# A two-block transformer in fp32: two of three 256-column products become one of 512 columns, and the bias rows move to the weight queue

## The chip, the cores and the metric

The kernel runs on one core of one Trainium2 chip. The metric is device time in microseconds (us). The core's engines work side by side, each in the order of its own queue: TensorE (PE) multiplies matrices, VectorE (DVE) and ScalarE (ACT) work element by element, GpSimd (POOL) does small sums and starts some transfers, and SyncE (SP) starts nearly all transfers of weights.

## The reference

Two transformer blocks run one after the other on x[1, 256, 1024] in fp32. The first has two layers, each with two feed-forward parts around an attention:

```python
def swiglu(h, w_in, w_out):
    g, u = jnp.split(h @ w_in, 2, axis=-1)
    return (jax.nn.silu(g) * u) @ w_out

# first block, in each of its two layers (FFN_HIDDEN = 2816)
h = modulate(rms_norm(x, norm_g[layer, 0]), sh1, sc1)
x = x + 0.5 * g1[:, None, :] * swiglu(h, ffn_w_in[layer, 0], ffn_w_out[layer, 0])
...
# layer 0: differential attention, whose logits get a bias per head by distance
bias = jnp.take(table, t5_bucket(rel), axis=0)
...
x = x + 0.5 * g3[:, None, :] * swiglu(h, ffn_w_in[layer, 1], ffn_w_out[layer, 1])
```

The second block mixes by convolutions, attends to a memory, and ends with product-key experts: each token picks its best experts by two top-k steps over query scores, and sums gelu(u_e . h) * gate * v_e over those it picked. The kernel computes u_e . h for all experts, 128 at a time, and drops what was not picked by one-hot products.

## The kernel before

Activations lie feature-major: x is [128, 8, 256], 8 tiles of 128 features by 256 tokens. An fp32 operand is split into two fp32r parts, hi and lo, and one product is three matmuls of 256 columns, which `mm3` (L145 to L149) issues for each 128x128 weight: whi with hi (L147), whi with lo (L148), wlo with hi (L149).

Weights come by `pieces` (L100 to L110): 1 MB from SP's queue into a tile `raw` (three buffers, two among the experts), which is split in two pieces of 128x1024. ScalarE copies out `whi` (L115), VectorE subtracts `wlo` (L116), and each piece is eight weights for PE. There are four buffers each of whi and wlo (three among the experts).

`ffn` (L431) is called four times; f0 stands before the attention of layer 0 and ends at about 260 us, f1 follows that attention, f2 and f3 belong to layer 1. Its first product goes over 22 hidden tiles j: one load, one piece for the gate `og`, one for `ou`, then silu (L450), the product `pr` (L452) and its split into `ghi` and `glo` (L160, L161). Its second product goes over 8 output tiles n with 22 triples each and adds the result to x (L426). Behind it `Stat.add` squares each new tile of x on ScalarE (`sq`, L182), adds it up on POOL (`sqa`, L193), and PE sums over the partitions (`po`, L177) for the next norm.

`prepare_bias` (L495 to L531) builds layer 0's bias tile TB while f0 runs: VectorE writes the eight heads' lines `mrow` (L509), and POOL's queue copies them to DRAM (`line`, L511), copies each line 128 times (`rows`, L515), and reads the rows back skewed by one element per partition into TB (L517). It is a generator, and `ffn` takes a step of it at some j (`next(beside)`).

Transfers `araw` (L355) and their sums on VectorE (L358) prepare the modulation of coming layers and run in the background of the FFNs.

With the experts, `experts_u` (L986) takes 128 experts in two halves, each expert's product (8 triples) evacuated by gelu (L1095 for the first 64). While the first 64 run, VectorE does the top-k of the tokens (L1020 to L1081) until about 1608 us. The last stage, from about 1902, multiplies by v with matmuls of 512 columns (L1171).

A scheduler sets the order in which the instructions of each engine stand; each engine then takes them in that order.

Of the kernel before, what the change touches and what calls it, by code (L numbers as in the profile page):

```python
# [10 lines left out]
F32 = mybir.dt.float32  # L11
# [42 lines left out]
def forward(ctx: ExitStack, tc: tile.TileContext, io, out, tap=None):  # L54
# [95 lines left out]

    def tok(h, k, a=0, b=T):

        return h[0][:, k, a:b], h[1][:, k, a:b]
# [65 lines left out]
    def h_tiles():  # L219
        return (hp.tile([128, KT, TE], F32R, tag="hhi", name="hi"), hp.tile([128, KT, TE], F32R, tag="hlo", name="lo"))  # L220

    class Norm:
# [3 lines left out]
        def __init__(self, a, b=None, h=None):  # L226
            self.a, self.b = a, b
            self.h = h_tiles() if h is None else h
            if b is not None and h is None:
                hi, lo = (t[:, :, T:TE] for t in self.h)  # L230
                bb = b.unsqueeze(2).to_broadcast([128, KT, 2])
                act.activation(hi, bb, AF.Copy)
                dve.tensor_tensor(lo, bb, hi, op=ALU.subtract)
# [51 lines left out]
    def fm_one(p, h, h32=None, n=T):  # L285
        o = mm_bank([128, n])
        for k in range(KT):
            if len(p) == 1:
                pe.matmul(o, p[0][:, k * 128:(k + 1) * 128], h32[:, k, :], start=(k == 0), stop=(k == KT - 1))  # L289
                continue  # L290
            mm3(o, blk(p, k), tok(h, k, 0, n), k == 0, k == KT - 1)
        return o
# [138 lines left out]
    def ffn(f, norm, gate, following, more=None, done=False):  # L431

        with tc.tile_pool(name="ff", bufs=1) as fp:
            ghi = fp.tile([128, FKT, T], F32R, name="ghi")
            glo = fp.tile([128, FKT, T], F32R, name="glo")
            src = io[f"ffn_in{f}"]
            h = norm.h
            for j in range(FKT):
                if f == 0 and j in (4, 6, 8, 10, 12, 14):
                    next(beside)  # L440
                it = W.pieces(src[j])
                if j == 0 and not done:
                    og, ou = norm.pair(next(it), next(it))
                elif j < 2:
                    og, ou = fm_pair(next(it), next(it), h)
                else:
                    og = fm_one(next(it), h)
                    ou = fm_one(next(it), h)
                sg = work("sil", [128, T], bufs=2)
                act.activation(sg, og, AF.Silu)  # L450
                pr = work("pr", [128, T], bufs=2)
                dve.tensor_tensor(pr, sg, ou, op=ALU.mult)  # L452
                split_into(ghi[:, j, :], glo[:, j, :], pr)
                tick()
# [14 lines left out]
            for n in range(KT):  # L469
                o = mm_bank([128, T])  # L470
                for k in range(FKT):
                    mm3(o, next(wb), (ghi[:, k, :], glo[:, k, :]), k == 0, k == FKT - 1)
# [15 lines left out]
    nlam = tbp.tile([128, 1], F32, name="nlam")  # L488
    g08 = tbp.tile([128, 1], F32, name="g08")
# [5 lines left out]
    def prepare_bias():  # L495
# [14 lines left out]
        line = dram.tile([8, 384], F32, name="line")  # L510
        pool.dma_start(out=line, in_=mrow)  # L511
        for q in range(4):
            yield
            rows = dram.tile([2, 128, 384], F32, name=f"rows{q}")
            pool.dma_start(out=rows, in_=line[2 * q:2 * q + 2, :].unsqueeze(1).to_broadcast([2, 128, 384]))  # L515

            pool.dma_start(out=TB[:, 2 * q:2 * q + 2, :],  # L517
# [462 lines left out]
    MID = 64  # L980
    with tc.tile_pool(name="pe0", bufs=1) as p0:
# [4 lines left out]
        def experts_u(e0, e1, evac):  # L986
            for c in range(e0 // 2, e1 // 2):
                for i, p in enumerate(W.pieces(io["peer_u"][c])):
                    evac(2 * c + i, fm_one(p, h))

        with tc.tile_pool(name="tk", bufs=1) as tk:
# [102 lines left out]
            def evac0(i, o):  # L1094
                act.activation(S0[:, i, :], o, AF.Gelu)  # L1095
# [11 lines left out]
        with tc.tile_pool(name="pe1", bufs=1) as p1:  # L1107
# [49 lines left out]
            xtok = hp.tile([128, 2, D], F32, tag="hhi", name="xtok")  # L1157
# [176 lines left out]
```

## Time and profile before

| what | value |
|---|---|
| median of 3 runs | 2270.47 us (2269.82 to 2273.29) |
| the profiled execution | 2270.32 us, its span 2268.5 us |
| PE, weight loads (PEld) | 98%, 94% of the span |
| VectorE, ScalarE, POOL | 77%, 55%, 4% |
| DMA | 467.76 MB, 206 GB/s in the mean |
| mean granted clock of TensorE | 0.996 |

The span goes from the first instruction to the last. A share is busy time by the span, over stages with different limits. An engine's row says how much it worked, not whether anything waited for it; for that one goes to the waits and to short windows.

### The profile page before, as it was taken

Reading aid. Unit: us, or ns where it says so; the run is one execution under the profiler, and the core shown is the slowest. Engines: PE = TensorE matmul, PEld = TensorE weight load, DVE = VectorE, ACT = ScalarE, POOL = GpSimd, SP = SyncE. Lnnn points to the kernel's source line nnn. Section 1 sums busy time; section 2 is a strip of 40 time slices with the busy share of each in tenths; the row PEclk is TensorE's granted clock in tenths of the full one; section 3 lists DMA queues with packets and bytes.
Section 4 is the critical chain, followed back from the end, with each engine's and each line's share of the span. In section 5 each row is a group of like instructions: output and inputs, shape, how many; then the busy total and the mean of one; then the engine's idle time right before and its main releaser. Section 6 shows DMA issues by size and latency. Waiting matters only on the chain.

```text
span 2268.5 us, 42687 instructions
## 1 busy us (share of the span) xinstructions
PE 2229.0 (98%) x16748; PEld 2131.5 (94%) x16748; DVE 1739.7 (77%) x3501; ACT 1258.6 (55%) x2389; POOL 85.3 (4%) x89
## 2 busy tenths in 40 slices
PE   8999899999999999999999999999999999999998
PEld 8999898999999999999999999999999999888887
DVE  7878667977777787765799886999668997666665
ACT  5544477544654457545523555445567776555555
POOL 0100000000100020000100010000000000000000
PEclk9999899999999999999999999999999999999999
DMA  9887644777668763555444453345543434555554
GB/s 364 297 325 300 231 168 164 301 275 293 245 263 300 292 231 129 216 182 182 164 159 165 161 219 115 117 184 186 186 155 144 145 136 152 193 192 188 185 187 157
DMA packets 68377, 467.76 MB, mean 206 GB/s; under 512 B 9888, under 2 KB 10184, under 8 KB 12368
## 3 DMA queue, kind: packets, MB, share of 16 engines
q1 hardware_dynamic: 64608, 461.67, 54.9%
q0 software_dynamic: 3280, 2.84, 0.5%
q8 instruction: 132, 2.16, 0.4%
q14 instruction: 69, 0.57, 0.1%
q10 hardware_dynamic: 288, 0.52, 0.1%
HBM read 463.88 MB, written 2.63 MB: 206 GB/s over the span
## 4 chain that ended last, share of the span: by engine, by line
PE 92%; DVE 3%; ACT 3%; issue 1%; POOL 0%; DMA 0%; ACTq 0%; DVEq 0%; POOLq 0%
PE mm L149 22%; PE mm L147 22%; PE mm L148 22%; PE mm L1171 8%; PE lg L1171 8%; PE lg L1126 2%; PE mm L289 2%; PE po L177 1%; ACT whi L115 1%; DVE wlo L116 1%; DVE lo L238 0%; DVE lo L275 0%; DVE nt L270 0%; PE po L962 0%; ACT e L576 0%
## 5 line engine op out<-in xcount | busy, mean ns | idle before, releaser
L115 ACT ACTIVATE whi<-raw 128x1024 fp32r<-128x1024 f32 x696 | 733.9, 1059 | 624.2 <-PE mm L148 414.6
L116 DVE TENSOR_TENSOR wlo<-raw,whi 128x1024 fp32r<-128x1024 f32 x696 | 850.5, 1226 | 295.8 <-ACT whi L115 291.0
L147 PE MATMUL mm<-hi,whi 128*128 128x256 f32 x3144 | 900.2, 287 | 2.6 <-ACT hi L274 2.1
L149 PE MATMUL mm<-hi,wlo 128*128 128x256 f32 x3144 | 892.7, 284 | 1.3 <-DVE wlo L116 1.2
L148 PE MATMUL mm<-lo,whi 128*128 128x256 f32 x3144 | 887.2, 282 | 0.1
L147 PEld LDWEIGHTS mm<-hi,whi 128*128 128x128 f32 x3144 | 595.2, 190 | 5.0 <-ACT hi L274 2.6
L149 PEld LDWEIGHTS mm<-hi,wlo 128*128 128x128 f32 x3144 | 596.4, 190 | 3.0 <-DVE wlo L116 2.7
L148 PEld LDWEIGHTS mm<-lo,whi 128*128 128x128 f32 x3144 | 596.9, 190 | 1.8 <-DVE wlo L116 0.6
L149 PE MATMUL mm<-ghi,wlo 128*128 128x256 f32 x704 | 197.4, 280 | 0.0
L147 PE MATMUL mm<-ghi,whi 128*128 128x256 f32 x704 | 197.4, 280 | 0.0
L148 PE MATMUL mm<-glo,whi 128*128 128x256 f32 x704 | 197.4, 280 | 0.0
L358 DVE CUSTOM_DVE_ANT_0 araw<-araw,cb 128x1024 f32<-128x1024 f32 x160 | 191.4, 1225 | 1.0 <-ACT cb L407 1.0
L160 ACT ACTIVATE vph<-S 128x128 fp32r<-128x128 f32 x256 | 77.1, 302 | 131.9 <-PE lg L1171 131.8
L148 PEld LDWEIGHTS mm<-glo,whi 128*128 128x128 f32 x704 | 132.7, 188 | 0.0
L147 PEld LDWEIGHTS mm<-ghi,whi 128*128 128x128 f32 x704 | 132.7, 188 | 0.0
L149 PEld LDWEIGHTS mm<-ghi,wlo 128*128 128x128 f32 x704 | 132.7, 188 | 0.0
L161 DVE TENSOR_TENSOR vpl<-S,vph 128x128 fp32r<-128x128 f32 x256 | 73.4, 288 | 44.3 <-PE lg L1171 43.8
L824 DVE SCALAR_TENSOR_TENSOR cfc<-cf,vec,cfc 128x256 f32<-128x256 f32 x240 | 100.0, 490 | 0.0
L1118 DVE TENSOR_SCALAR ohA<-cst,sel 128x128 f32<-128x128 f32 x256 | 82.2, 342 | 21.8 <-PE lg L1126 20.8
L1171 PE MATMUL mm<-whi,vph 128*128 128x512 f32 x256 | 80.7, 395 | 0.2 <-ACT vph L160 0.2
L1171 PE MATMUL mm<-wlo,vph 128*128 128x512 f32 x256 | 80.9, 395 | 0.0
L1171 PE MATMUL lg<-whi,vpl 128*128 128x512 f32 x256 | 80.8, 395 | 0.0
(392 smaller groups left out, 3277.7 us busy)
## 6 DMA issues: line engine op xcount, KB each, us to landing
raw<-ffn_in SPq DMA_DIRECT2D x88, 1024.0 KB, 4.9
araw<-ada SPq DMA_DIRECT2D x72, 1024.0 KB, 6.9
raw<-peer_u SPq DMA_DIRECT2D x64, 1024.0 KB, 4.8
raw<-peer_v SPq DMA_DIRECT2D x64, 1024.0 KB, 4.8
raw<-ffn_out SPq DMA_DIRECT2D x44, 1024.0 KB, 4.8
araw<-kv_ada SPq DMA_DIRECT2D x8, 1024.0 KB, 6.8
raw<-w_cf SPq DMA_DIRECT2D x8, 1024.0 KB, 4.7
raw<-w_scx SPq DMA_DIRECT2D x8, 1024.0 KB, 4.8
```

The source lines that it names most:

```text
L115: act.activation(hi[:, :m], r, AF.Copy)
L116: last_split[0] = dve.tensor_tensor(lo[:, :m], r, hi[:, :m], op=ALU.subtract)
L147: pe.matmul(o, a[0], b[0], start=start, stop=False)
L148: pe.matmul(o, a[0], b[1], start=False, stop=False)
L149: pe.matmul(o, a[1], b[0], start=False, stop=stop)
L160: act.activation(pair_hi, src, func, **kw)
L161: dve.tensor_tensor(pair_lo, src, pair_hi, op=ALU.subtract)
L289: pe.matmul(o, p[0][:, k * 128:(k + 1) * 128], h32[:, k, :], start=(k == 0), stop=(k == KT - 1))
L358: dve.tensor_tensor_reduce(out=raw[:, i, :], in0=raw[:, i, :], in1=cb, scale=1.0, scalar=0.0, op0=ALU.mult, op1=ALU.add, accum_out=acc[:, ...
L824: dve.scalar_tensor_tensor(o, cf[:, i, j:j + T], w, o, op0=ALU.mult, op1=ALU.add)
L1118: dve.tensor_scalar(A, iota, sel3[:, 0, t:t + 1], sel3[:, 2, t:t + 1], op0=ALU.is_equal, op1=ALU.mult)
L1171: pe.matmul(acc[t][d], lh, rh[:, d * 512:(d + 1) * 512], start=s0, stop=s1)
```

## The change

`mm_wide` replaces `mm3` where hi and lo can lie side by side: one matmul of 512 columns takes whi with [hi | lo] into a bank [128, 2, 256], and one of 256 columns adds wlo with hi to its first half. The halves are then added in SBUF: ScalarE copies one out of PSUM, VectorE adds the other. It is used for j from 2 to 20 of each FFN's first product, for n from 0 to 6 of its second (there a second residual step on VectorE adds the half), and for experts 16 to 62. The operands h and g become one tile each with both halves. In `prepare_bias` the copy to DRAM (`line`) is left out: each `rows` is read straight from one partition of mrow, 128 times, by two transfers of 192 KB, on SP's queue, and so is each read into TB. The steps are taken at j from 3 to 12. The small tiles nlam and g08 move to another pool.

```text
lines of after that stand in the rows below:
L105 weight load, L369 araw, L549 rows, L553 TB, L115/L116 whi/wlo, L468 copy of og's half, L470 silu,
L471 copy of ou's half, L166 g (the hi part), L188 sq, L244 next operand
```

```diff
@@ -147,6 +147,12 @@
         pe.matmul(o, a[0], b[0], start=start, stop=False)
         pe.matmul(o, a[0], b[1], start=False, stop=False)
         pe.matmul(o, a[1], b[0], start=False, stop=stop)
+
+    def mm_wide(o, a, b, start, stop):
+
+        order = ((o, a[0], b), (o[:, 0, :], a[1], b[:, 0]))
+        for i, (oo, w, r) in enumerate(order if start else order[::-1]):
+            pe.matmul(oo, w, r, start=start and i == 0, stop=stop and i == 1, skip_group_check=True)
 
     def tok(h, k, a=0, b=T):
 
...
@@ -289,6 +296,13 @@
                 pe.matmul(o, p[0][:, k * 128:(k + 1) * 128], h32[:, k, :], start=(k == 0), stop=(k == KT - 1))
                 continue
             mm3(o, blk(p, k), tok(h, k, 0, n), k == 0, k == KT - 1)
+        return o
+
+    def fm_wide(p, h):
+
+        o = mm_bank([128, 2, T])
+        for k in range(KT):
+            mm_wide(o, blk(p, k), h[2][:, :, k, 0:T], k == 0, k == KT - 1)
         return o
 
     def proj_fm(W, name, h, consume, c0=0, c1=None, whole=(), h32=None, ahead=None, norm=None, wide=False):
@@ -431,26 +445,36 @@
     def ffn(f, norm, gate, following, more=None, done=False):
 
         with tc.tile_pool(name="ff", bufs=1) as fp:
-            ghi = fp.tile([128, FKT, T], F32R, name="ghi")
-            glo = fp.tile([128, FKT, T], F32R, name="glo")
+            g = fp.tile([128, FKT, 2, T], F32R, name="g")
             src = io[f"ffn_in{f}"]
             h = norm.h
             for j in range(FKT):
-                if f == 0 and j in (4, 6, 8, 10, 12, 14):
+                if f == 0 and 3 <= j <= 12:
                     next(beside)
                 it = W.pieces(src[j])
                 if j == 0 and not done:
                     og, ou = norm.pair(next(it), next(it))
                 elif j < 2:
                     og, ou = fm_pair(next(it), next(it), h)
-                else:
+                elif j == FKT - 1:
                     og = fm_one(next(it), h)
                     ou = fm_one(next(it), h)
+                else:
+                    og = fm_wide(next(it), h)
+                    ou = fm_wide(next(it), h)
                 sg = work("sil", [128, T], bufs=2)
-                act.activation(sg, og, AF.Silu)
                 pr = work("pr", [128, T], bufs=2)
-                dve.tensor_tensor(pr, sg, ou, op=ALU.mult)
-                split_into(ghi[:, j, :], glo[:, j, :], pr)
+                if 2 <= j < FKT - 1:
+                    act.activation(sg, og[:, 1, :], AF.Copy)
+                    dve.tensor_tensor(sg, og[:, 0, :], sg, op=ALU.add)
+                    act.activation(sg, sg, AF.Silu)
+                    act.activation(pr, ou[:, 1, :], AF.Copy)
+                    dve.tensor_tensor(pr, ou[:, 0, :], pr, op=ALU.add)
+                    dve.tensor_tensor(pr, sg, pr, op=ALU.mult)
+                else:
+                    act.activation(sg, og, AF.Silu)
+                    dve.tensor_tensor(pr, sg, ou, op=ALU.mult)
+                split_into(g[:, j, 0, :], g[:, j, 1, :], pr)
                 tick()
             tc.keep_in_program_order(act.preload_act_table(AF.Sqrt))
             s = mod(gate)
@@ -467,9 +491,17 @@
 
             wb = stream()
             for n in range(KT):
-                o = mm_bank([128, T])
+                two = n < KT - 1
+                o = mm_bank([128, 2, T] if two else [128, T])
                 for k in range(FKT):
-                    mm3(o, next(wb), (ghi[:, k, :], glo[:, k, :]), k == 0, k == FKT - 1)
+                    if two:
+                        mm_wide(o, next(wb), g[:, k], k == 0, k == FKT - 1)
+                    else:
+                        mm3(o, next(wb), (g[:, k, 0, :], g[:, k, 1, :]), k == 0, k == FKT - 1)
+                if two:
+                    dve.scalar_tensor_tensor(xT[:, n, :], o[:, 1, :], s[:, n:n + 1], xT[:, n, :],
+                                             op0=ALU.mult, op1=ALU.add)
+                    o = o[:, 0, :]
                 residual(n, o, s[:, n:n + 1], st, nxt)
                 if more is not None:
                     more.add(xT[:, n, :], scale=v("final_g", n))
@@ -485,8 +517,8 @@
     tbp = ask.enter_context(tc.tile_pool(name="tb", bufs=1))
     dram = ask.enter_context(tc.tile_pool(name="dr", bufs=1, space=bass.MemoryType.DRAM))
     TB = tbp.tile([128, 8, 256], F32, name="TB")
-    nlam = tbp.tile([128, 1], F32, name="nlam")
-    g08 = tbp.tile([128, 1], F32, name="g08")
+    nlam = const.tile([128, 1], F32, name="nlam")
+    g08 = const.tile([128, 1], F32, name="g08")
     qz = [tbp.tile([128, 2, 256], F32, name=f"qz{i}") for i in range(4)]
     for t in qz:
         pool.memset(t[64:128, 0, :], 0.0)
@@ -507,14 +539,18 @@
         pf = bank("lg", [8, 384])
         pe.matmul(pf, rb, oh, start=True, stop=True)
         dve.scalar_tensor_tensor(mrow, pf, -1.0, mrow, op0=ALU.mult, op1=ALU.add)
-        line = dram.tile([8, 384], F32, name="line")
-        pool.dma_start(out=line, in_=mrow)
+        copies = []
         for q in range(4):
             yield
             rows = dram.tile([2, 128, 384], F32, name=f"rows{q}")
-            pool.dma_start(out=rows, in_=line[2 * q:2 * q + 2, :].unsqueeze(1).to_broadcast([2, 128, 384]))
-
-            pool.dma_start(out=TB[:, 2 * q:2 * q + 2, :],
+            copies.append(rows)
+            for i in range(2):
+                hd = 2 * q + i
+                sync.dma_start(out=rows[i:i + 1], in_=mrow[hd:hd + 1, :].unsqueeze(1).to_broadcast([1, 128, 384]))
+        for q, rows in enumerate(copies):
+            yield
+
+            sync.dma_start(out=TB[:, 2 * q:2 * q + 2, :],
                            in_=bass.AP(tensor=rows.tensor, offset=rows.offset + 127,
                                        ap=[[383, 128], [128 * 384, 2], [1, 256]]))
         yield
@@ -978,6 +1014,7 @@
     wsk.close()
     NI = 128
     MID = 64
+    WIDE = 16
     with tc.tile_pool(name="pe0", bufs=1) as p0:
         W = Weights(pw, 2, 3)
         S0 = p0.tile([128, MID, T], F32, name="S0")
@@ -986,7 +1023,8 @@
         def experts_u(e0, e1, evac):
             for c in range(e0 // 2, e1 // 2):
                 for i, p in enumerate(W.pieces(io["peer_u"][c])):
-                    evac(2 * c + i, fm_one(p, h))
+                    e = 2 * c + i
+                    evac(e, fm_wide(p, h) if WIDE <= e < MID - 1 else fm_one(p, h))
 
         with tc.tile_pool(name="tk", bufs=1) as tk:
             wkp[0] = tk
@@ -1092,6 +1130,11 @@
             proj_fm(W, "w_peer_q", h, q_evac, norm=norm)
 
             def evac0(i, o):
+                if WIDE <= i < MID - 1:
+                    t = work("sum", [128, T], bufs=2)
+                    act.activation(t, o[:, 1, :], AF.Copy)
+                    dve.tensor_tensor(t, o[:, 0, :], t, op=ALU.add)
+                    o = t
                 act.activation(S0[:, i, :], o, AF.Gelu)
                 if qs:
                     scores()
```

Three places show how the order of the engines' rows moved. First SP's queue in f0's first product, after the change. The weight loads of j4 to j7 are raw_1060, raw_1117, raw_1178 and raw_1242.

```order
29 L105 DMA raw_1060<-ffn_in0 128x2048
30 L549 DMA rows0_1057<-mrow_798 128x1x384 x2
31 L549 DMA rows1_1114<-mrow_798 128x1x384 x2
32 L105 DMA raw_1117<-ffn_in0 128x2048
33 L369 DMA araw_1171<-ada0 128x2048
34 L549 DMA rows2_1175<-mrow_798 128x1x384 x2
35 L105 DMA raw_1178<-ffn_in0 128x2048
36 L369 DMA araw_1232<-ada0 128x2048
37 L549 DMA rows3_1239<-mrow_798 128x1x384 x2
38 L105 DMA raw_1242<-ffn_in0 128x2048
39 L553 DMA TB_736<-rows0_1057 128x2x256
40 L105 DMA raw_1297<-ffn_in0 128x2048
```

Before, in the same place (j4 is raw_1085, then raw_1151, raw_1224 and raw_1297):

```order
29 L105 DMA raw_1085<-ffn_in0 128x2048
30 L105 DMA raw_1151<-ffn_in0 128x2048
31 L355 DMA araw_1217<-ada0 128x2048
32 L105 DMA raw_1224<-ffn_in0 128x2048
33 L355 DMA araw_1290<-ada0 128x2048
34 L105 DMA raw_1297<-ffn_in0 128x2048
35 L105 DMA raw_1366<-ffn_in0 128x2048
```

The eight reads of mrow now stand ahead of the loads of j5, j6 and j7; before, SP's queue held only raw and araw there.

Second, ScalarE's row in f0. After the change, raw_1117 is the load of j5 and raw_1178 that of j6; sil_1104 and pr_1105 evacuate j4, sil_1161 and pr_1162 evacuate j5.

```order
88 L468 ACTIVATE sil_1104<-mm_1066 128x256
89 L470 ACTIVATE sil_1104<-sil_1104 128x256
90 L471 ACTIVATE pr_1105<-mm_1087 128x256
91 L166 ACTIVATE g_804<-pr_1105 128x256
92 L115 ACTIVATE whi_1119<-raw_1117 128x1024
93 L115 ACTIVATE whi_1140<-raw_1117 128x1024
94 L468 ACTIVATE sil_1161<-mm_1123 128x256
95 L470 ACTIVATE sil_1161<-sil_1161 128x256
96 L471 ACTIVATE pr_1162<-mm_1144 128x256
97 L166 ACTIVATE g_804<-pr_1162 128x256
98 L115 ACTIVATE whi_1180<-raw_1178 128x1024
99 L115 ACTIVATE whi_1201<-raw_1178 128x1024
```

Before, raw_1151 is the load of j5 and raw_1224 that of j6; sil_1070 and ghi with pr_1072 evacuate j3, sil_1145 and ghi with pr_1147 evacuate j4:

```order
82 L115 ACTIVATE whi_1153<-raw_1151 128x1024
83 L450 ACTIVATE sil_1070<-mm_1016 128x256
84 L115 ACTIVATE whi_1182<-raw_1151 128x1024
85 L160 ACTIVATE ghi_805<-pr_1072 128x256
86 L115 ACTIVATE whi_1226<-raw_1224 128x1024
87 L450 ACTIVATE sil_1145<-mm_1091 128x256
88 L115 ACTIVATE whi_1255<-raw_1224 128x1024
89 L160 ACTIVATE ghi_805<-pr_1147 128x256
```

Before, the splits of a j alternate with the evacuation of the j two before it; after, those of j5 and of j6 stand behind the whole evacuation of the j just before them, and those of j7 likewise.

Third, ScalarE's row at the end of f0's second product; sq is the square of a new tile of x, hi (and h) the operand of the next product. Before:

```order
139 L182 ACTIVATE sq<-xT 128x256
140 L237 ACTIVATE hi<-xT,mod_sc_2271 128x256
141 L115 ACTIVATE whi<-raw 128x1024 x3
142 L237 ACTIVATE hi<-xT,mod_sc_2271 128x256
143 L115 ACTIVATE whi<-raw 128x1024 x2
...
149 L115 ACTIVATE whi<-raw 128x1024 x3
150 L237 ACTIVATE hi<-xT,mod_sc_2271 128x256
151 L115 ACTIVATE whi<-raw 128x1024 x2
152 L182 ACTIVATE sq<-xT 128x256 x5
153 L198 ACTIVATE rstd<-po,eps_c 128x2
```

After:

```order
175 L115 ACTIVATE whi<-raw 128x1024 x3
176 L188 ACTIVATE sq<-xT 128x256
177 L244 ACTIVATE h<-xT,mod_sc_2043 128x256
178 L115 ACTIVATE whi<-raw 128x1024 x3
179 L188 ACTIVATE sq<-xT 128x256
180 L244 ACTIVATE h<-xT,mod_sc_2043 128x256
181 L115 ACTIVATE whi<-raw 128x1024 x3
182 L188 ACTIVATE sq<-xT 128x256
183 L244 ACTIVATE h<-xT,mod_sc_2043 128x256
184 L115 ACTIVATE whi<-raw 128x1024 x2
185 L188 ACTIVATE sq<-xT 128x256
186 L244 ACTIVATE h<-xT,mod_sc_2043 128x256
```

Before, three sq stand by their own n and five behind the last whi; after, each of the eight stands by its own n. In POOL's row the transfers of rows and TB, which before stood ahead of and between the sqa, are gone.

## Rows read from the trace of the kernel before

**Rows 1.** The page: busy time, chain that ended last, costliest groups.

```profile
PE 2229.0 (98%) x16748; PEld 2131.5 (94%) x16748; DVE 1739.7 (77%) x3501; ACT 1258.6 (55%) x2389; POOL 85.3 (4%) x89
...
PE 92%; DVE 3%; ACT 3%; issue 1%; POOL 0%; DMA 0%; ACTq 0%; DVEq 0%; POOLq 0%
PE mm L149 22%; PE mm L147 22%; PE mm L148 22%; PE mm L1171 8%; PE lg L1171 8%; PE lg L1126 2%; PE mm L289 2%; PE po L177 1%; ACT whi L115 1%; DVE wlo L116 1%; DVE lo L238 0%; DVE lo L275 0%; DVE nt L270 0%; PE po L962 0%; ACT e L576 0%
...
L116 DVE TENSOR_TENSOR wlo<-raw,whi 128x1024 fp32r<-128x1024 f32 x696 | 850.5, 1226 | 295.8 <-ACT whi L115 291.0
```

**Rows 2.** Busy us (x count) of PE, PEld, DVE, ACT, POOL; PEclk; DMA share; GB/s.

```profile
150.00:200.00 50.00, 50.00 (x420) 50.00 (x419) 38.10 (x56) 23.91 (x36) 0.00 (x0) 1.00 0.79 295
200.00:260.00 60.00, 60.00 (x517) 60.00 (x516) 47.15 (x63) 28.10 (x35) 3.00 (x3) 1.00 0.77 291
570.00:589.00 19.00, 19.00 (x162) 19.00 (x161) 13.19 (x16) 8.96 (x11) 2.05 (x3) 1.00 0.63 235
2000.00:2050.00 50.00, 50.00 (x217) 40.55 (x216) 30.94 (x54) 28.06 (x55) 0.00 (x0) 1.00 0.54 190
```

**Rows 3.** The same view, behind f0, f1 and f2, and inside the first.

```profile
260.30:287.20 26.90, 17.01 (x110) 15.89 (x109) 16.33 (x33) 9.52 (x20) 5.47 (x4) 0.75 0.34 134
589.90:603.40 13.50, 13.48 (x111) 13.22 (x111) 12.59 (x32) 8.27 (x17) 7.04 (x2) 1.00 0.49 192
831.00:845.60 14.60, 13.59 (x111) 13.12 (x110) 13.23 (x26) 8.17 (x15) 7.25 (x3) 1.00 0.59 221
266.10:274.20 8.10, 0.29 (x4) 0.08 (x2) 6.26 (x7) 3.62 (x7) 5.47 (x4) 0.71 0.76 307
269.50:282.00 12.50, 5.75 (x20) 4.84 (x21) 7.07 (x14) 3.01 (x8) 4.39 (x4) 0.50 0.22 85
```

**Rows 4.** Waits between 255 and 290 us: total, times, longest.

```profile
POOL sqa L193 <- ACT sq L182: 44.1, 1, 44.1
...
PE po L177 <- POOL sqa L193: 7.8, 1, 7.8
```

**Rows 5.** ScalarE's timeline in f0's first product: start, duration, instruction [idle before it].

```profile
98.41 1.06 ACT L115 ACTIVATE whi<-raw 128x1024 fp32r<-128x1024 f32 x1 [1.50 <-issue]
...
101.29 1.06 ACT L115 ACTIVATE whi<-raw 128x1024 fp32r<-128x1024 f32 x1 [1.55 <-PE mm L148]
104.15 1.06 ACT L115 ACTIVATE whi<-raw 128x1024 fp32r<-128x1024 f32 x1 [1.50 <-issue]
```

**Rows 6.** Groups by line, 70 to 260 us: busy, mean ns, idle before.

```profile
L452 DVE TENSOR_TENSOR pr<-sil,mm 128x256 f32<-128x256 f32 x22 | 9.2, 416 | 6.0 <-PE mm L149 5.6 <-ACT sil L450 0.5
L160 ACT ACTIVATE ghi<-pr 128x256 fp32r<-128x256 f32 x22 | 8.8, 400 | 0.0
L450 ACT ACTIVATE sil<-mm 128x256 f32<-128x256 f32 x22 | 8.0, 365 | 0.0
...
L426 DVE SCALAR_TENSOR_TENSOR xT<-mm,mod_gt,xT 128x256 f32<-128x256 f32 x7 | 3.4, 479 | 1.5 <-PE mm L149 1.5
```

**Rows 7.** Busy time by stretch: f0, f1, experts with the top-k.

```profile
1525.00:1608.00 83.00, 83.00 (x700) 83.00 (x700) 77.08 (x139) 44.99 (x65) 0.00 (x0) 1.00 0.50 179
...
75.00:198.00 123.00, 122.97 (x1021) 122.00 (x1021) 98.51 (x151) 61.76 (x90) 7.13 (x8) 1.00 0.87 318
425.00:525.00 100.00, 100.00 (x837) 100.00 (x837) 77.37 (x114) 46.75 (x71) 0.00 (x0) 1.00 0.81 301
```

**Rows 8.** The instruction that writes mrow.

```profile
L509 DVE SCALAR_TENSOR_TENSOR mrow<-lg,mrow x1: 539/539/539, 83.1 to 83.1; 8x384 f32<-8x384 f32 x1
```

**Rows 9.** A stretch in which the DMA engines were full, the same view.

```profile
615.60:618.10 2.50, 2.50 (x24) 2.01 (x23) 1.80 (x2) 1.82 (x3) 0.00 (x0) 1.00 1.01 410
```

**Rows 10.** DMA issues: count, KB each, median us to landing.

```profile
raw<-ffn_in SPq DMA_DIRECT2D x88, 1024.0 KB, 4.9
...
kA<-FT SPq DMA_DIRECT2D x1, 16.0 KB, 2.2
```

**Rows 11.** The stretch in which kA<-FT ran, the same view.

```profile
627.00:627.30 0.30, 0.30 (x4) 0.30 (x4) 0.00 (x0) 0.30 (x3) 0.00 (x0) 1.00 0.23 55
```

More of the change, by code (lines that the diff above doesn't have):

```diff
@@ L219, in h_tiles @@
     def h_tiles():
-        return (hp.tile([128, KT, TE], F32R, tag="hhi", name="hi"), hp.tile([128, KT, TE], F32R, tag="hlo", name="lo"))
+        t = hp.tile([128, 2, KT, TE], F32R, tag="h", name="h")
+        return t[:, 0], t[:, 1], t
     class Norm:
@@ L229, in __init__ @@
             if b is not None and h is None:
-                hi, lo = (t[:, :, T:TE] for t in self.h)
+                hi, lo = (t[:, :, T:TE] for t in self.h[:2])
                 bb = b.unsqueeze(2).to_broadcast([128, KT, 2])
@@ L1154, in forward @@
                 done[0] += 1
-            xtok = hp.tile([128, 2, D], F32, tag="hhi", name="xtok")
+            xtok = hp.tile([128, 2, D], F32, tag="h", name="xtok")
             for t in range(2):
```

## The prediction

> **What bounds the kernel now.** I read the page first: TensorE (PE) is busy 98% of the span, and in the chain that ended last it has 92%, nearly all of it the three products of an fp32 triple, L147 to L149 [rows 1]. So time goes only in three ways: a shorter PE step, less idle PE, or new idle PE. Second, the step. A matmul record lasts 0.28 us at a step of 0.12 us, so about two of a window's count lie over its edge, and I take two off. In an FFN's first product that gives 50/418 = 119.6 ns, in f0's second 60/515 = 116.5, in f1's second 19/160 = 118.8; a matmul of 512 columns, in the last stage, 50/215 = 232.6 ns, which is 2 x 116.3 [rows 2]. The experts have 83/698 = 118.9 [rows 7]. Third, the idle. The largest piece lies behind f0: from the last FFN product, 260.3, the next two pairs of products take 26.9 us, where they take 13.5 behind f1 and 14.6 behind f2; between 266.1 and 274.2 PE has 0.29 us of work, and then runs at a granted clock of 0.50, its lower level (1.2 of 2.4 GHz), until 282 [rows 3]. The waits name the cause: PE's sum of squares (po, L177) waits 7.8 us for POOL's sqa (L193), and POOL had waited 44.1 us for ScalarE's sq (L182) [rows 4]. In the order of before, five sq stand behind the last weight split. Last, the cover: in f0 weights are split some 6 us before PE wants them: j4's last product ends at about 101.25, where the second split of j6 is released by it, and the first one of j6 started at 98.41 [rows 5].
>
> **The change, part by part.**
>
> *The wait behind f0.* In the order of after, the sq of each n stands right behind its own residual, as in f1, and no bias transfer stands in POOL's row. The stretch should take what f1 and f2 take: 26.9 - 13.5 or - 14.6 = 12.3 to 13.4 us. I take a gain of **12.7**.
>
> *Wide products.* 4 x 19 x 16 = 1216 triples of the first products, 4 x 7 x 22 = 616 of the second (154 of them f0's), 47 x 8 = 376 of the experts become one matmul of 512 and one of 256 columns: 2208 in all. If the wide one keeps the last stage's step and the narrow one its own, a triple saves 2 x 119.6 - 232.6 = 6.6 ns in the first products, 5.0 in f1 to f3's second and the experts, 0.4 in f0's second: 8.0 + 2.3 + 1.9 + 0.1 = 12.3 us. At the least it saves nothing: f0's second product runs 256 columns at 116.5, so the columns and not the number of instructions set the pace, and what makes 119.6 elsewhere may stay; the forecast would then be 2285. If the narrow one also falls to 116.3, a triple takes 348.9 and the sum is 18.4 us. No row decides between them, so I take **7.5**, a little over half of 12.3.
> The Trainium skill, "TensorE: Matmul & The Clock Gate", section "Back-to-back issue gap", gives each matmul its columns and a fixed small gap of about 2.5 ns. By it each merged pair would save that gap, 2208 x 2.5 = 5.5 us as an estimate; the trace's 232.6 against 2 x 116.5 shows no such gap.
>
> *Halves added.* In the FFNs a j gets two more copies on ScalarE and two more adds on VectorE (0.42 us each, as pr [rows 6]). VectorE stands at 98.5 of 123 us in f0 and 77.4 of 100 in f1; with 0.84 us in each 5.7 that becomes 93% and 92% [rows 7]. It stays below full and is covered by the splits' lead: **0.5 us** lost (0 to 24, see the rivals). The second residual step on VectorE, 28 x 0.48 us (L426 [rows 6]), lies under 15 us of PE work each: nothing.
> With the experts the cover is gone. From 1525 to 1608 VectorE, with the top-k, is busy 77.1 of 83 us [rows 7]. In it, 29 experts (16 to 44) get an add from PSUM of 0.42 us, as pr: 12.1 us, so 89.2 us must go into 83. What is late is wlo, and so PE: some 6 us; I take **6.5** lost (3, if the top-k ends some experts later, to 10).
>
> *The order in f0.* In after, ScalarE's splits for j5, j6 and j7 stand behind the whole evacuation of the j before. When PE ends j4, nothing is split for j5: copy 0.36, add 0.42, product 0.42, g 0.40, then whi 1.06, of which PE can use one matmul before wlo (1.22 later) [rows 1, 5, 6]: 2.7 + 0.9 = 3.6 us of idle PE, three times: **10.8 us lost** at the least. Behind f0 a gap of 8 us was followed by 12 us at the lower clock [rows 3]; these gaps are shorter, and I add 1 us for each, 3 (0 to 5).
>
> *Bias rows on the weight queue.* Eight reads, each 128 times one 1.5 KB line of one partition of mrow (192 KB), now stand in SP's queue: four ahead of j5's weights, two ahead of j6's, two of j7's. mrow is done at 83.1 + 0.5 [rows 8], and j4's weights have to pass too: they start at about 84. Behind them up to j7 are three weight loads and two ada loads, each 1.05 MB / 0.41 = 2.56 us at the most that the queues moved [rows 9]: 12.8 us. Then 2.2 us to landing, as of a 16 KB transfer [rows 10], and whi and wlo, 2.1. With R for one read, j7 can start at 84 + 8R + 12.8 + 2.2 + 2.1 = 101.1 + 8R. Without stalls it would at 101.25 + 2 x 5.75 = 112.7 (5.74 from the first split of j6 to that of j7 [rows 5]). The stall up to j7 is 8R - 11.6, where this is more than the 10.8 of the order; the two run at once, so the larger counts. They part at R = 2.8 us.
> R stands nowhere in the trace. Below, 192 KB at 410 GB/s: 0.5 us. Above, if one partition gives no more than one of the 16 DMA engines moves, 410/16 = 26 GB/s: 7.7 us. The nearest row is a transfer that holds to one partition, kA<-FT, 16 KB into one: the queues moved 55 GB/s in the 0.3 us in which it ran [rows 11]. At that, R = 196.6/55 = 3.6 us, and the stall is 17.0 us. I take it, with 3.5 us for the clock.
> The four TB transfers (256 KB, 0.6 us each at 410 GB/s) come behind, when the splits have a lead of 5.7 us again: nothing. Their cover gone, they would cost 2.6.
>
> **Sum**, against the profiled run's 2270.32 us (2268.5 of span and 1.8 around; the median of the runs is 2270.47): -12.7 - 7.5 + 0.5 + 6.5 = -13.2; + 17.0 + 3.5 = +7.3: **2277.6 us**.
>
> **Rivals.**
> A, the reads are quick (R under 2.8): only the order counts, -13.2 + 10.8 + 3 = +0.6, 2270.9 us. For it speaks that 16 KB may show a lag and not a pace.
> B, faster: the narrow matmul falls to the last stage's pace as well, and the wide products save 18.4 us and not 7.5. With quick reads that is +0.6 - 10.9 = -10.3, 2260.0 us; it decides from a saving of 12.6 us on, which brings A's sum to 4.5 us under before. For it: f0's second product (116.5) and the last stage (232.6) show that the pace can be had for either width. Against it: three of four FFN products, and the experts, don't run at it with the same instructions.
> C, one partition gives 26 GB/s: R = 7.7, stall 50 us, clock 5: +41.8, 2312 us. The Trainium skill, "SBUF — State Buffer", section "Door 1: The DMA port swizzle", measures 27.6 GB/s for transfers held to partitions 0 to 3, one port; by it R would be 7.1 us and the time 2307, as estimates. The 55 GB/s of kA speaks against it, though for writes of a twelfth of the size.
> D, VectorE becomes the pace of the FFNs: at 92 to 93%, if one of the two adds of a j falls out of the cover, 57 j of f0 to f2 cost 57 x 0.42 = 24 us. With A, 2294 us. For it: wlo already waits for whi; against it: the lead of two pieces.
>
> **How the numbers follow.** The forecast has 0.34, A 0.18, B 0.30, C 0.12, D 0.06. The time is the forecast's, 2277.6. From 2256 (B, with the top-k at 3) to 2308 (just under C's upper end) about 0.85 is held; by itself the forecast has 2270 to 2290 (R from 2.8 to 5). About 0.2%, 4.5 us, is what a measurement of this kernel can tell from no change. Slower has most of the forecast, C and D: 0.47; same A and the forecast's low end, 0.21; faster B and a little of A, 0.32.
>
> **What the profile after would show.** If the reads hold the queue: to landing of some 4 us or more each, ScalarE's whi waiting for DMA between 98 and 130, and PE idle ahead of j5, j6 and j7; if only the order counts, three gaps of 3.6 us with whi waiting for ScalarE's own row. Behind f0 the two pairs should take 13 to 15 us with no wait for sqa. In the FFNs, a wide step near 232 ns, narrow 116 to 120. In the top-k stage, wlo ahead of PE's waits and VectorE over 95%. The forecast is wrong if R is under 2.8 us, or if the FFNs run steadily slower or faster than the 349 to 359 ns of a triple.

## The result, and the profile after

The changed kernel takes **2285.26 us** (median of 4 runs, 2283.78 to 2285.69) against 2271.38 for the kernel before, run beside it (2269.82 to 2273.29): a ratio of 1.006, with a 95% interval of 1.0042 to 1.0077. It is slower by some 14 us, inside the range and on the side that was forecast (2277.6), but by twice the forecast 7 us. The profiled execution took 2284.82 us with a span of 2283.0, 14.5 over that of before.

The page of the kernel after, its busy times and its chain, to set beside [rows 1]:

```profile
PE 2218.3 (97%) x14540; PEld 2020.9 (89%) x14540; DVE 1822.4 (80%) x3728; ACT 1328.1 (58%) x2588; POOL 82.3 (4%) x80
...
PE 87%; DVE 6%; ACT 3%; DMA 2%; issue 1%; POOL 0%; ACTq 0%; DVEq 0%; POOLq 0%; SPq 0%
PE mm L155 31%; PE mm L149 10%; PE mm L147 10%; PE mm L148 10%; PE mm L1214 8%; PE lg L1214 8%; PE lg L1169 2%; PE mm L296 2%; DMA raw<-ffn_in 2%; DVE wlo L116 2%; ACT whi L115 1%; PE po L183 1%; DVE h L282 0%; DVE h L245 0%; DVE nt L277 0%
```

PE has 2208 matmuls fewer and less busy time, and yet the span grew: the chain has lost 5% of PE to others, 2% of it a transfer of weights, raw<-ffn_in, where transfers had 0% before. So PE stood idle, and the waits say where. Waits of the kernel after from 60 to 260 us (engine and line, what it waited for, total us, times, longest):

```profile
PE mm L155 <- ACT whi L115: 31.2, 6, 17.4
...
ACT whi L115 <- DMA raw<-ffn_in: 23.1, 4, 14.4
```

PE waited 31.2 us for whi in f0, and ScalarE, which makes whi, 23.1 for the weights (raw). What the transfers did meanwhile stands in stretches of f0, in the columns of [rows 2]:

```profile
84.00:96.00 12.00, 12.00 (x71) 10.41 (x70) 9.66 (x20) 7.98 (x15) 0.00 (x0) 1.00 0.86 27
111.50:118.00 6.50, 1.27 (x2) 0.74 (x3) 1.44 (x2) 2.00 (x2) 0.00 (x0) 0.50 1.00 339
118.00:126.00 8.00, 7.18 (x31) 6.01 (x30) 3.94 (x7) 1.19 (x3) 0.00 (x0) 0.75 0.86 31
126.00:132.00 6.00, 0.00 (x0) 0.00 (x0) 0.97 (x3) 0.77 (x2) 0.00 (x0) 0.73 0.97 316
132.00:141.00 9.00, 8.09 (x29) 6.65 (x30) 5.41 (x9) 2.46 (x4) 0.00 (x0) 0.61 0.90 107
```

From 84 to 96 the DMA engines are 86% busy and move 27 GB/s: these are the reads of mrow. When they are through, the weights come at 339 GB/s while PE stands still (1.27 of 6.5 us), at the lower clock (a granted clock of 0.50); then two more reads, and the same again. In three stretches PE works at the lower clock:

```profile
101.50:122.00 20.50, 5.27 (x15) 4.26 (x16) 4.65 (x6) 2.00 (x2) 0.00 (x0) 0.50 0.91 127
128.80:139.00 10.20, 6.09 (x18) 4.88 (x19) 4.99 (x8) 2.00 (x2) 0.00 (x0) 0.50 0.94 195
145.80:152.70 6.90, 5.03 (x15) 4.01 (x16) 4.36 (x4) 4.01 (x4) 0.00 (x0) 0.51 0.99 392
```

That is 16.4 us of work, about half of which, 8 us, is the price of the clock (an estimate: the level is half of the other). VectorE's split of g (L167) dates each j; its timeline from j4 to j8 (start, duration):

```profile
101.06 0.43 DVE L167 TENSOR_TENSOR g<-pr,g 128x256 fp32r<-128x256 f32 x1 [0.48 <-ACT g L166]
...
127.06 0.43 DVE L167 TENSOR_TENSOR g<-pr,g 128x256 fp32r<-128x256 f32 x1 [0.48 <-ACT g L166]
...
143.64 0.43 DVE L167 TENSOR_TENSOR g<-pr,g 128x256 fp32r<-128x256 f32 x1 [0.48 <-ACT g L166]
...
157.87 0.42 DVE L167 TENSOR_TENSOR g<-pr,g 128x256 fp32r<-128x256 f32 x1 [0.48 <-ACT g L166]
...
164.19 0.41 DVE L167 TENSOR_TENSOR g<-pr,g 128x256 fp32r<-128x256 f32 x1
```

The same split (L161) started in before at 103.5, 109.3, 115.0, 120.8 and 126.5; the first and the last of them:

```profile
103.53 0.42 DVE L161 TENSOR_TENSOR glo<-pr,ghi 128x256 fp32r<-128x256 f32 x1
...
126.51 0.42 DVE L161 TENSOR_TENSOR glo<-pr,ghi 128x256 fp32r<-128x256 f32 x1
```

So j4 was 2.5 us early, and j5 to j8 were 17.8, 28.6, 37.1 and 37.7 late: 40.2 us were lost from j4 to j8, 31.2 of them in waits and about 8 by the clock. Part of it came back. The busy times behind f0, in f1's first and second product, with the top-k, and in the last stage, to set beside [rows 2], [rows 3] and [rows 7]:

```profile
297.00:310.40 13.40, 13.38 (x111) 13.12 (x110) 11.27 (x27) 8.31 (x17) 0.00 (x0) 1.00 0.51 193
475.00:525.00 50.00, 50.00 (x286) 43.27 (x285) 45.27 (x76) 30.44 (x54) 0.00 (x0) 1.00 0.80 292
555.00:585.00 30.00, 30.00 (x175) 26.40 (x174) 25.15 (x33) 14.13 (x20) 3.90 (x3) 1.00 0.75 275
1540.00:1624.00 84.00, 81.00 (x450) 68.03 (x449) 81.34 (x160) 51.37 (x88) 0.00 (x0) 1.00 0.48 165
2000.00:2050.00 50.00, 50.00 (x220) 41.03 (x219) 31.55 (x56) 28.28 (x55) 0.00 (x0) 1.00 0.55 190
```

The two pairs behind f0 take 13.4 us where they took 26.9 [rows 3]. In f1's first product 284 matmuls (two less than the count) are 142 wide pairs in 50 us, 352 ns for what three of 119.6 did in 359; in its second 173 in 30 us, 347 ns. With the top-k VectorE is at 97% and PE no longer full. In the last stage, whose code is the same, 218 matmuls of 512 columns pass in 50 us and not 215 [rows 2].

The whole of the 14.5 us, by dated instructions of both traces (us, after less before):

| stretch | forecast | measured |
|---|---|---|
| up to j4 of f0 | 0 | -2.5 |
| j4 to j8, the held queue, order and clock | +20.5 | +40.2 |
| the rest of f0 | | -1.0 |
| the wait behind f0 | -12.7 | -13.6 |
| from there to the same place behind f3 | | -8.8 |
| from there to the last stage, with the experts | +6.5 | +5.4 |
| the last stage, from its first matmul | 0 | -5.2 |

The forecast had -7.5 for the wide products and +0.5 for their adds in all stretches together.

### The profile page after: what moved, and what is told of

The parts are those of the page before. It is cut to its first block, busy times and chain, and to the rows that moved or that the text cites. A ratio compares the mean times of both kernels' runs of the same rounds, so it can differ in the third digit from the quotient of the medians.

```text
span 2283.0 us, 38606 instructions
## 1 busy us (share of the span) xinstructions
PE 2218.3 (97%) x14540; PEld 2020.9 (89%) x14540; DVE 1822.4 (80%) x3728; ACT 1328.1 (58%) x2588; POOL 82.3 (4%) x80
## 4 chain that ended last, share of the span: by engine, by line
PE 87%; DVE 6%; ACT 3%; DMA 2%; issue 1%; POOL 0%; ACTq 0%; DVEq 0%; POOLq 0%; SPq 0%
PE mm L155 31%; PE mm L149 10%; PE mm L147 10%; PE mm L148 10%; PE mm L1214 8%; PE lg L1214 8%; PE lg L1169 2%; PE mm L296 2%; DMA raw<-ffn_in 2%; DVE wlo L116 2%; ACT whi L115 1%; PE po L183 1%; DVE h L282 0%; DVE h L245 0%; DVE nt L277 0%
## 5 line engine op out<-in xcount | busy, mean ns | idle before, releaser
L155 PE MATMUL mm<-h,whi 128*128 128x512 f32 x1592 | 555.1, 401 | 31.2 <-ACT whi L115 31.2
L147 PE MATMUL mm<-h,whi 128*128 128x256 f32 (+1 forms) x1552 | 449.9, 291 | 0.7 <-ACT h L281 0.6
L149 PE MATMUL mm<-h,wlo 128*128 128x256 f32 (+1 forms) x1552 | 441.2, 285 | 1.2 <-DVE wlo L116 0.9
L148 PE MATMUL mm<-h,whi 128*128 128x256 f32 (+1 forms) x1552 | 438.4, 283 | 0.6 <-DVE h L282 0.5
L155 PE MATMUL mm<-h,wlo 128*128 128x256 f32 x1592 | 418.7, 283 | 3.8 <-DVE wlo L116 3.7
L155 PEld LDWEIGHTS mm<-h,whi 128*128 128x128 f32 x1592 | 290.7, 191 | 90.2 <-ACT whi L115 33.7
L155 PEld LDWEIGHTS mm<-h,wlo 128*128 128x128 f32 x1592 | 302.6, 191 | 23.7 <-DVE wlo L116 8.1
L148 PEld LDWEIGHTS mm<-h,whi 128*128 128x128 f32 x1552 | 293.6, 189 | 2.8 <-DVE h L282 1.9
L149 PEld LDWEIGHTS mm<-h,wlo 128*128 128x128 f32 x1552 | 293.7, 189 | 2.5 <-DVE wlo L116 2.1
L147 PEld LDWEIGHTS mm<-h,whi 128*128 128x128 f32 x1552 | 293.6, 189 | 2.3 <-ACT h L281 0.8
L155 PE MATMUL mm<-g,whi 128*128 128x512 f32 x616 | 213.5, 393 | 0.0
L155 PE MATMUL mm<-g,wlo 128*128 128x256 f32 x616 | 168.0, 280 | 0.0
L155 PEld LDWEIGHTS mm<-g,whi 128*128 128x128 f32 x616 | 113.9, 188 | 23.9
L155 PEld LDWEIGHTS mm<-g,wlo 128*128 128x128 f32 x616 | 116.0, 188 | 2.3
L167 DVE TENSOR_TENSOR vpl<-S,vph 128x128 fp32r<-128x128 f32 x256 | 73.6, 290 | 38.1 <-PE lg L1214 38.0
```

What stands on the lines that cost most here:

```text
L147: pe.matmul(o, a[0], b[0], start=start, stop=False)
L148: pe.matmul(o, a[0], b[1], start=False, stop=False)
L149: pe.matmul(o, a[1], b[0], start=False, stop=stop)
L155: pe.matmul(oo, w, r, start=start and i == 0, stop=stop and i == 1, skip_group_check=True)
L167: dve.tensor_tensor(pair_lo, src, pair_hi, op=ALU.subtract)
```

## The experiments

The theory was that the eight reads, each of one partition, are slow and hold the weight queue. Its rivals: the packets are slow from wherever they are read; the wide products or the order of ScalarE's row lose the time.

**The shift of the tiles alone.** The change also moves two small tiles to another pool, and with them the tiles that lie behind them in SBUF. The 64 bytes, and the 32 of a later run, are reckoned from the layout; no view shows addresses. In the kernel before:

```diff
-    nlam = tbp.tile([128, 1], F32, name="nlam")
-    g08 = tbp.tile([128, 1], F32, name="g08")
+    nlam = const.tile([128, 1], F32, name="nlam")
+    g08 = const.tile([128, 1], F32, name="g08")
```

> The kernel before, with one thing of the change: the small tiles nlam and g08 lie in the other pool, so that all later tiles lie 64 bytes further on. Theory: the last stage, whose code is unchanged, fell from 232.4 to 228.9 ns per matmul of 512 columns by this shift alone; then its step is 229 here, the stage is 4.8 us shorter, f0's second product goes from 116.5 to about 118 ns and that of f1 to f3 from 118.8 to about 117.3, and the time is 4 to 8 us under before (2263 to 2267). Rival: the last stage gained by something else that the change does (another order, other transfers); then the step stays 232.4 and the time within 2 us of before.

It took 2266.57 us against 2270.68, a ratio of 0.9981 (0.9972 to 0.999). Its windows, in f0's second product, in f1's, and in the last stage:

```profile
200.00:258.00 58.00, 58.00 (x492) 58.00 (x492) 44.83 (x62) 26.48 (x33) 3.01 (x3) 1.00 0.76 284
571.00:589.00 18.00, 18.00 (x154) 18.00 (x153) 12.38 (x15) 8.39 (x11) 1.81 (x2) 1.00 0.65 240
2000.00:2050.00 50.00, 50.00 (x220) 41.00 (x220) 31.05 (x55) 28.85 (x56) 0.00 (x0) 1.00 0.53 191
```

The last stage has 218 matmuls in 50 us (229.4 ns), as the kernel after, and f0's second product 58/490 = 118.4 ns in place of 116.5. f1's, 18/152 = 118.4, did not fall to 117.3. From its first matmul to its last, the last stage takes 353.2 us and not 358.5, while the stages up to it take 1.5 us more. So the shift gives some 4 us, and it gives them in the last stage.

**The wide products alone.** The kernel after, with `line`, `rows` and TB on POOL's queue, and their steps at the j, as in before:

```diff
-                if f == 0 and 3 <= j <= 12:
+                if f == 0 and j in (4, 6, 8, 10, 12, 14):
...
+        line = dram.tile([8, 384], F32, name="line")
+        pool.dma_start(out=line, in_=mrow)
...
-                sync.dma_start(out=rows[i:i + 1], in_=mrow[hd:hd + 1, :].unsqueeze(1).to_broadcast([1, 128, 384]))
...
+            pool.dma_start(out=rows, in_=line[2 * q:2 * q + 2, :].unsqueeze(1).to_broadcast([2, 128, 384]))
```

> The kernel after, with the bias rows back on POOL's queue as before: the wide products alone (with the shift of the tiles). Theory, that the weight queue held behind the eight reads of mrow: the 40 us between j4 and j8 are gone, the wait behind f0 is back (13.7), so 14.5 - 40.1 + 13.7 + 2.4 = 9.5 us under before, about 2262. Rival, that the wide products and their additions lengthen f0: some 20 us and more of the loss stay between j4 and j8 and the time is above 2271.

2259.16 us, a ratio of 0.9949 (0.9934 to 0.9964). From 60 to 300 us PE's sum of squares (po) waits 7.8 us for sqa, as in [rows 4], and PE never waits for whi; its longest waits:

```profile
PE po L183 <- POOL sqa L199: 7.8, 1, 7.8
PE mm L147 <- ACT h L281: 2.1, 2, 1.5
```

The wide products lose nothing in f0: its last product ends at 257.6 us, where it ended at 260.6 before.

**The bias rows alone.** The kernel before, with the new `prepare_bias` and its steps at j from 3 to 12:

```diff
-                if f == 0 and j in (4, 6, 8, 10, 12, 14):
+                if f == 0 and 3 <= j <= 12:
...
-        line = dram.tile([8, 384], F32, name="line")
-        pool.dma_start(out=line, in_=mrow)
...
+                sync.dma_start(out=rows[i:i + 1], in_=mrow[hd:hd + 1, :].unsqueeze(1).to_broadcast([1, 128, 384]))
```

> The kernel before, with only the bias rows moved to the weight queue, all products as before. Theory of the held queue: 40.1 us lost between j4 and j8, 2.4 won ahead of it, 13.7 won behind f0: 24 us over before, about 2295; reads of mrow run at 27 to 28 GB/s, 7.0 us each. Rival, the order of ScalarE's rows with wide products made the loss: 10 to 14 us lost at j5 to j7, 13.7 won, about 2270.

2295.38 us, a ratio of 1.0107 (1.0091 to 1.0122): 24.7 us lost, as the theory had it. Its wait in f0 and the stretch of the first reads:

```profile
PE mm L147 <- ACT whi L115: 31.8, 7, 16.8
...
84.00:96.00 12.00, 12.00 (x102) 12.00 (x101) 9.02 (x16) 7.83 (x13) 0.00 (x0) 1.00 0.85 27
```

PE waits 31.8 us for whi, from 84 to 96 the queues move 27 GB/s again, and the two pairs behind f0 take 13.4 us. So this part alone makes the loss and the gain behind f0. ScalarE's new order comes with it too: its row there has whi of j5 (116.43) behind the whole evacuation of j4 (ghi, 101.27), after 14.7 us of waiting for the transfer.

**The same reads from 16 partitions.** The kernel after; the small product writes each head's line into 16 partitions, eight apart, and a read takes its 128 copies from them:

```diff
-        mrow = tbp.tile([8, 384], F32, name="mrow")
+        mrow = tbp.tile([128, 384], F32, name="mrow")
...
-                sync.dma_start(out=rows[i:i + 1], in_=mrow[hd:hd + 1, :].unsqueeze(1).to_broadcast([1, 128, 384]))
+                sync.dma_start(out=rows[i].rearrange("(r s) c -> r s c", s=8),
+                               in_=mrow[hd:128:8, :].unsqueeze(1).to_broadcast([16, 8, 384]))
```

> The kernel after, with each head's line in 16 partitions, eight apart (mrow is 128 x 384, the small product writes each line 16 times), and each read taking its 128 copies from these 16: same bytes, same packets, same queue, same order. Theory, that the one partition limits the read: a read falls from 7.0 us to 1 us or less, the stretch moves above 100 GB/s, the loss between j4 and j8 falls from 40 to what the order leaves, 11 to 14 us, and the time is 2257 to 2261. Rival, that packets of 1.5 KB or the writes into DRAM on this queue are slow by themselves: the stretch stays near 28 GB/s and the time near 2285.

2261.47 us, a ratio of 0.9958 (0.9943 to 0.9973), just over the upper end of what was expected. The stretch of its reads, and that behind it:

```profile
84.40:88.40 4.00, 4.00 (x25) 3.48 (x24) 4.00 (x7) 3.97 (x7) 0.00 (x0) 1.00 1.07 229
100.00:130.00 30.00, 20.55 (x81) 16.23 (x80) 18.95 (x29) 11.58 (x18) 0.00 (x0) 0.80 0.54 197
```

The reads now pass at 229 GB/s, and rows<-mrow lands in 6.0 us in the median and not 20.7. Same bytes, same packets, same queue: what made them slow was that each had its source in one partition (whether the partition itself is the limit, or a port that several share, this run does not separate). Between j4 and j7 16.3 us are still lost, 2 more than the 11 to 14 expected, with three gaps in which PE waits for whi (9.4 us) and ScalarE's row shows whi in its new place behind g, with no wait for a transfer before it:

```profile
101.84 0.42 ACT L166 ACTIVATE g<-pr 128x256 fp32r<-128x256 f32 x1 [0.95 <-DVE pr L473]
102.17 1.99 ACT L115 ACTIVATE whi<-raw 128x1024 fp32r<-128x1024 f32 x2
...
112.83 0.42 ACT L166 ACTIVATE g<-pr 128x256 fp32r<-128x256 f32 x1 [0.95 <-DVE pr L473]
113.15 1.99 ACT L115 ACTIVATE whi<-raw 128x1024 fp32r<-128x1024 f32 x2
...
123.47 0.42 ACT L166 ACTIVATE g<-pr 128x256 fp32r<-128x256 f32 x1 [0.95 <-DVE pr L473]
123.79 3.88 ACT L115 ACTIVATE whi<-raw 128x1024 fp32r<-128x1024 f32 x4
```

The 16.3 are the difference of the splits of g, 1.2 us early at j4 and 15.1 late at j7. From 100 to 130 the granted clock is 0.80 in the mean: in three stretches at 0.50 PE did 13.1 us of work (3.4, 3.2 and 6.5), half of which, some 6.5 us, is the clock's share (an estimate).

**The reads on POOL's queue.** The kernel after, with the slow reads, and TB, on another queue:

```diff
-                sync.dma_start(out=rows[i:i + 1], in_=mrow[hd:hd + 1, :].unsqueeze(1).to_broadcast([1, 128, 384]))
+                pool.dma_start(out=rows[i:i + 1], in_=mrow[hd:hd + 1, :].unsqueeze(1).to_broadcast([1, 128, 384]))
...
-            sync.dma_start(out=TB[:, 2 * q:2 * q + 2, :],
+            pool.dma_start(out=TB[:, 2 * q:2 * q + 2, :],
```

> The kernel after, with the same eight reads from one partition of mrow each, and the TB reads, on POOL's queue and no longer on the weight queue. Theory, that a slow read holds only what stands behind it on its own queue: the reads still take about 7 us each, 84 to 140 us, but the weights pass at their pace, PE doesn't wait for whi in f0 (under 2 us), five sq stand behind the last whi again, and the time is that of the wide products alone, 2257 to 2261. Rival, that the reads hold the DMA engines for all queues: weights land late in f0, PE waits 15 us and more there, time above 2272.

2298.99 us, a ratio of 1.0127 (1.011 to 1.0144): the rival was right. Its waits from 60 to 260 us:

```profile
ACT whi L115 <- DMA raw<-ffn_in: 46.6, 2, 43.5
...
PE mm L155 <- DVE pr L472: 38.3, 1, 38.3
```

ScalarE's timeline at that place, with the idle time before the instruction in brackets:

```profile
140.90 1.06 ACT L115 ACTIVATE whi<-raw 128x1024 fp32r<-128x1024 f32 x1 [43.53 <-DMA raw<-ffn_in]
```

And the stretch of the reads, in the columns of [rows 2], with what each queue had of it (packets, MB, share of the 16 DMA engines; q0 is POOL's, q1 SP's):

```profile
85.00:140.00 55.00, 20.35 (x116) 17.34 (x114) 14.18 (x26) 9.82 (x17) 3.99 (x7) 0.70 0.97 97
...
q0 software_dynamic: 593, 1.86, 81.3%
q1 hardware_dynamic: 476, 3.45, 15.4%
```

The wait of PE is put down to VectorE's pr, which had only to wait its turn: ScalarE's row shows the cause, whi waiting 43.5 us for a transfer on the other queue. From 85 to 140 the DMA engines are 97% busy and move 97 GB/s in the mean, and POOL's queue has 81% of their time for the smaller part of the bytes. So a place in the weight queue is not needed for the loss: here the slow reads held the DMA engines from another queue. (On POOL's queue the trace has the reads in packets of 3 and 4.6 KB; so packets of 1.5 KB are not what makes them slow.)

**Spread reads on POOL's queue, TB on the weight queue.** The kernel of the spread reads, with the reads on POOL's queue, which also brings back ScalarE's order of before:

```diff
-                sync.dma_start(out=rows[i].rearrange("(r s) c -> r s c", s=8),
+                pool.dma_start(out=rows[i].rearrange("(r s) c -> r s c", s=8),
```

> The kernel after, with the lines spread over 16 partitions as in the run before, the reads of mrow on POOL's queue and only the TB reads on the weight queue. In its order the splits of j5 to j7 stand ahead of the evacuations again, and all eight sq by their own n. Theory, that the order of ScalarE's row makes the 16 us left in f0 with the spread lines, and the five late sq the wait behind f0: neither is there, 2259.2 - 13.7 = 2245.5, 2243 to 2248. Rival, that the 16 us come from the weights' being late behind TB and rows: 10 us and more of them stay, 2255 or above.

2244.47 us, a ratio of 0.9885 (0.9869 to 0.9902). From 60 to 300 us no wait of PE is longer than 0.6 us, neither for whi nor for sqa. In the spread reads on the weight queue whi never waited for a transfer from 60 to 260 us, so it was the order that made the 16.3 us.

**And no adds beside the top-k.** The same, with the experts 16 to 45 as triples again:

```diff
-    WIDE = 16
+    WIDE = 46
```

> As the run with lines spread, reads on POOL's queue and TB on the weight queue, and the experts 16 to 45 as 256-column triples again, so that no add stands beside the top-k. Theory, that VectorE is full there: the 5.5 us lost between 1519 and 1657 us in the run with the wide products alone are not lost, 2239 to 2242. Rival, that they are lost to the wide products' own step or to ScalarE's copies: within 2 us of the same kernel with wide experts.

**2240.06 us**, a ratio of 0.9867 (0.9851 to 0.9884), under both kernels. It is 4.4 us under the run before it. The same stretch in that run and in this one:

```profile
1500.00:1584.00 84.00, 80.91 (x448) 68.02 (x447) 81.38 (x158) 51.32 (x89) 0.00 (x0) 1.00 0.47 165
...
1500.00:1584.00 84.00, 84.00 (x708) 84.00 (x707) 77.50 (x135) 45.59 (x68) 0.00 (x0) 1.00 0.52 176
```

VectorE falls from 97% to 92% and PE is full. In the run before, PE waits 3.0 us for VectorE's wlo between 1510 and 1645, in this one never. The edit takes out the wide products, ScalarE's copies and VectorE's adds at once, so it does not tell adds from copies: VectorE itself waited 15.1 us for the copies there.

**A shift of 32 bytes.** The first experiment left open by what rule the shift acts; this moved nlam alone, in the kernel before:

```diff
-    nlam = tbp.tile([128, 1], F32, name="nlam")
+    nlam = const.tile([128, 1], F32, name="nlam")
```

> The kernel before, with only nlam in the other pool: all later tiles lie 32 bytes further on, and the operands of most products, 96 bytes over a multiple of 128 before, lie on a multiple. Theory, that the step depends on where the operand lies and is short on the multiple (f0's second product, whose ghi lay on one, had 116.5 ns, the others 118.8 to 119.6): the first products of the FFNs fall to about 116.5, 4 x 1056 x 3.1 ns = 13 us less there, the last stage to 229 or under, and the time is 2250 to 2256, while f0's second product rises to 118. Rival, that 64 bytes matter by another rule (the last stage alone): first products stay at 119 to 120 and the time within 5 us of before.

2273.39 us, a ratio of 1.001 (1.0001 to 1.002). A miss for the theory: the first products kept 50/418 = 119.6 ns, f0's second went to 58/483 = 120.1, the last stage to 50/214 = 233.6:

```profile
150.00:200.00 50.00, 50.00 (x420) 50.00 (x419) 38.73 (x57) 24.02 (x37) 0.00 (x0) 1.00 0.78 297
200.00:258.00 58.00, 58.00 (x485) 58.00 (x485) 45.22 (x62) 26.39 (x32) 3.01 (x3) 1.00 0.73 279
2000.00:2050.00 50.00, 50.00 (x216) 40.23 (x215) 30.39 (x54) 28.14 (x54) 0.00 (x0) 1.00 0.53 187
```

## Why the prediction was right, and where it was off

The direction and the mechanism held: the reads stand ahead of the weights of j5 to j7 and PE waits for whi. The bias rows alone give +24.7 us, the rest of the change -11.5.

*Bias rows on the weight queue.* This term was mis-sized: 31.2 us of waits for a forecast 17.0, and about 8 us by the clock for 3.5. The step that failed is "The nearest row is a transfer that holds to one partition, kA<-FT": 55 GB/s, R = 3.6 us for one read. The reads moved 27 GB/s, so R is 196.6/27 = 7.3 us, close to the upper bound of 7.7 by the pace of one DMA engine: that is rival C's mechanism. By 8R - 11.6 that would be 47 us; the loss from j4 to j8, clock and order in it, was 40.2. The likely reason is that the last reads ran beside other transfers (107 GB/s from 132 to 141); it is not shown. The Trainium skill, "SBUF — State Buffer", section "Door 1: The DMA port swizzle", has 27.6 GB/s for transfers held to partitions 0 to 3; here the trace agrees, 27 GB/s for the reads of the first partitions. Perhaps the 16 KB of kA were too short a row to show a pace (rival A's objection, turned the other way), or writes differ from reads; no run tells.

The prediction also counted only what stands behind the reads in their own queue. The reads on POOL's queue show that weights of another queue wait as well.

*The order in f0.* With quick reads it cost 16.3 us, 9.4 in waits for whi and some 6.5 by the clock, against 10.8 + 3: the clock was put too low here too. With the reads on POOL's queue and spread, the order of before comes back and the loss goes: this mechanism is shown. The order came with the reads on the weight queue and not with the wide products, as the two runs with one part each show. In the kernel after it lay under the larger stall, as "the larger counts" says.

*The wait behind f0.* -13.6 for -12.7. In every run the wait stayed where five sq stand last, and went where each stands by its own n.

*Wide products.* -7.5 was too little. f1 to f3 with their surroundings gave 8.8 us and f0 1.0, at 6.7 ns a triple in f1's first product (359 to 352) and 9.6 in its second (356.4 to 346.8), so the first sum of 12.3 was nearer. That the 6.6 ns of its first products came true was luck: it had the wide step at 232.6 ns and the narrow one still at 119.6, but by the starts of the matmuls in f1's first product a wide one takes 235 ns and a narrow one 117. The narrow one fell nearly as rival B had it, and the wide one did not keep the last stage's pace. The share of the experts isn't measured by itself.

*Halves added.* PE waited 0.8 us for wlo in f1 and not at all in f2 and f3: rival D did not happen. With the top-k, 4.4 us were won by leaving the wide form out, its own saving set off, against 6.5 forecast and in its bounds; whether the adds or the copies cost it is open.

*The last stage* and the start of f0 stood in no term: -5.2 and -2.5. The first is the shift of the tiles; the second was not followed up. With the gains that came out larger than forecast they hid 12.5 of the 19.7 us by which the term of the rows was too small; so the time came out nearer to the forecast than its sum deserved. That closeness was luck.

## What to carry to other kernels

Read a repeated line from many partitions, not from one, even for small transfers: reads of 192 KB took some 7 us each here, and 0.9 (by the pace of their stretch) when their source lay in 16 partitions, which alone gave back 24 us. Another queue did not hide the slow reads, which had 81% of the DMA engines' time from there; look for a stretch with busy DMA engines and few GB/s. And a merged product that needs a copy and an add belongs where those engines have room: the same merge paid in the FFNs and lost beside the top-k, where VectorE was at 97%.

## What the runs showed of the hardware

Reads of one partition, 1.5 KB a packet, moved 27 GB/s with the engines 86% busy; the same packets from 16 partitions 229 GB/s. A queue of its own did not keep such reads from delaying weights of another by 43.5 us.

The step of matmuls that no edit touches depends on where tiles lie in SBUF: in the last stage 232.6 ns in before, 233.6 with a shift of 32 bytes and 229.4 with 64; in f0's second product 116.5, 120.1 and 118.4. All seven kernels with the two tiles moved have the last stage at 353.2 us; the kernel before and the bias rows alone have it at 358.5. The first products did not move (119.6 ns at 0, 32 and 64 bytes). A rule by multiples of 128 bytes was forecast and did not hold; which operand or which access it is stays open.
